# An encoder layer in split float32 on one core: weights' low parts made on GpSimd, the convolution's running sum in PSUM, the MLP's buffers in another order

## The chip, the cores and the metric

The kernel runs on one core of a Trainium2 chip. The metric is device microseconds of one execution, lower is better. Engines are named as in the profile: PE (TensorE), DVE (VectorE), ACT (ScalarE), POOL (GpSimd) and SP (SyncE), whose queue issues most DMAs.

## The reference, cut to what matters

One layer of an encoder over 512 tokens of 1024 channels, in float32. Three branches read the same normalised input, are weighted by sigmoid gates, summed, projected and added to the input; a squared-ReLU MLP follows.

```python
h = rms_norm(x, norm_mix_pre)
za, zb, q, k, v, su, sv, gl = split(h @ w_in)             # w_in: 1024 x 10240
a = za * sigmoid(zb)
a = depthwise_conv(a, conv_w) + conv_b                    # 31 taps per channel
y_a = silu(layer_norm(a, conv_ln_g, conv_ln_b)) @ w_proj_conv
y_b = rms_norm(diff_attention(q, k, v, lam, slopes)) @ w_proj_attn      # 8 heads
gv = layer_norm(gelu(sv)); y_c = (gelu(su) * (sgu_w @ gv + sgu_b)) @ w_proj_sgu
g_a, g_b, g_c = split(sigmoid(gl + b_gate))
x = x + rms_norm((g_a * y_a + g_b * y_b + g_c * y_c) @ w_out, norm_mix_post)
h = rms_norm(x, norm_ffn_pre)
x = x + rms_norm(square(relu(h @ w_ffn_up)) @ w_ffn_down, norm_ffn_post)
```

## The kernel before, in words

**Split operands.** Every float32 operand of a matmul is kept as two float32r tiles, a high part (the value rounded) and a low part (the value minus the high part). A product is three matmuls, high x high, high x low and low x high, in `mm3`. A *unit* is one PSUM bank of 128 x 512 results from one weight tile: 8 steps of the inner dimension, 24 matmuls. All matmuls of the program carry line L58 in the profile, all transposes L62.

**Weights.** The list `specs` names the 148 weight tiles of 512 KB each in the order in which they are used; here they are counted from 0. `load_to` does three things for each: a DMA on SP's queue into `w_raw` (L156), the high part on ACT (L157), the low part on DVE (L158, two inputs in SBUF). `w_raw`, `w_hi` and `w_lo` have three buffers each, so a high part can be written when PE is done with the tile three places earlier. `take(m)` loads two tiles beyond those that it hands out. In the first half of the program the tiles are: 0 to 3 the gated linear units (GLU) of the first two channel blocks, 4 and 5 the values of the first pair of heads, 6 and 7 queries and keys of head 0, up to 39 the rest of attention and the GLU, 40 to 47 `sv`, 48 to 63 `w_proj_attn` with its gates, 64 to 71 `su`, 72 to 87 `w_proj_sgu` with its gates, 88 to 93 six of the convolution's gates, and 94 to 103 `w_proj_conv` with the last two gates. Then come `w_out`, four tiles of `w_ffn_up`, and `w_ffn_down`.

**Order of the work.** PE's instructions are kept in program order. The other engines' order is set by a list scheduler over the program order; each engine then works strictly in its order, and a waiting instruction holds up all that stand behind it. The convolution runs on DVE beside everything else: `conv_taps` goes through the channel blocks, and for each makes a first product (L361) and 30 multiply-adds (L366) on a running sum `acc`, 128 x 512, in one SBUF buffer; `conv` hands out a number of these steps with a low priority.

**PSUM.** There are eight banks. `banks(ph, 4)` makes a pool with four banks with tag `a`, for the units, and four with tag `b`, for transposes, scores and small products. `bank(tag)` takes the next of its tag in turn; PE waits if the bank's last reader is not done.

**Stages.** (1) Norm, transposes, and three units in the banks `fb[0]`, `fb[1]`, `fb[2]`, in two halves of the tokens; then the sigmoid of `fb[0]` on ACT (`glu_gate`, L386), whose product with `fb[1]` is DVE's `glu_out` (L390); then a fourth unit. Beside them POOL zeroes the borders of the convolution's input (L353, L354), loads four small vectors for the attention's lambda (`bcast`, L194) and makes the distances for ALiBi (`iota`, L428). (2) Attention: for each head the scores and softmax run in step with the units of the next head, which are `proj_qk` (two units; DVE writes the low half of the keys at L459), `proj_v` for every second head, and late GLUs. A head's key unit is read twice by ACT (L458) and twice by DVE (L459) before its bank is free. (3) `sv`, with the attention's outputs turned beside it. (4) `merge` over `w_proj_attn`, the gating unit, `merge` over `w_proj_sgu`. (5) Layer norm of the convolution (`conv_norm`), its SiLU (`conv_silu`, ACT L753 and L754, DVE L755) and `merge` over `w_proj_conv`. (6) `w_out`, norms, and the first four tiles of `w_ffn_up` (`PLAIN`). (7) The rest of `w_ffn_up` as blocked products with seven multiplications in place of eight: `load_block` issues the DMAs (L909), `operand` makes sums and their two parts (ACT L930, DVE L931), `side` and `parts` make the sums of the other operand in the tile `ring` (ACT L882, DVE L883). (8) `w_ffn_down` and the last norm.

**Memory.** `fp` is the pool of stages 7 and 8. It is laid over the tiles of the pools that were closed before, in the order in which its tiles first appear: `gpo`, `f` (64 KB per partition), `ring` (33 KB), `r`, the six block buffers `aq`, `sn`. A tile waits until every older tile at its addresses has been read for the last time.

Of the kernel before, what the change touches and what calls it, by code (L numbers as in the profile page):

```python
# [16 lines left out]
P = 128  # L17
S = 512
# [30 lines left out]
def encoder_layer(ctx: ExitStack, tc: tile.TileContext, a: dict, out: bass.AP):  # L49
# [14 lines left out]
    def mk(name, bufs=1, **kw):  # L64
        return tc.tile_pool(name=name, bufs=bufs, reuse_waits="tile", **kw)

    def f32(ap):
        return ap.bitcast(F32)
# [10 lines left out]
    def cols(n, c0):  # L79
        return wv[n][:, :, c0:c0 + P]  # L80
# [39 lines left out]
    for n in range(KT):  # L120
        specs += [cols("w_in", GL + n * P)] if n >= EARLY else []
        specs += [cols("w_proj_conv", n * P)]
    xp = {"pool": None, "set": range(len(specs) + 4, len(specs) + 9)}
    for nh in range(2):
        specs += [rows("w_out", k, nh * 512) for k in range(0, KT, 2)]
# [20 lines left out]
    def load_to(n):  # L146
        while len(loaded) < min(n, gate_at[0]):
            if len(loaded) in xp["set"] and xp["pool"] is None:
                break
            src = specs[len(loaded)]  # L150
            m = src.shape[2]
            raw = wp.tile([P, 1024], F32, tag="raw", bufs=3, name="w_raw")
            p, n_ = (xp["pool"], 5) if len(loaded) in xp["set"] else (wp, 3)
            hi = p.tile([P, 1024], F32R, tag="hi", bufs=n_, name="w_hi")
            lo = p.tile([P, 1024], F32R, tag="lo", bufs=n_, name="w_lo")
            nc.sync.dma_start(raw.rearrange("p (k c) -> p k c", c=m), src)  # L156
            act.activation(hi, raw, AF.Copy)  # L157
            vec.tensor_tensor(lo, raw, f32(hi[:, :]), op=ALU.subtract)  # L158
            loaded.append((hi.rearrange("p (k c) -> p k c", c=m), lo.rearrange("p (k c) -> p k c", c=m)))

    def take(m=1, ahead=2):
        i = taken[0]
        taken[0] += m
        load_to(i + m + ahead)
        return loaded[i:i + m]
# [4 lines left out]
    hp = ctx.enter_context(mk("hp"))  # L170
    ps = {"pool": None, "a": 4, "b": 4}

    def banks(stack, na):

        ps.update(pool=stack.enter_context(mk(f"ps{na}", space=PSUM)), a=na, b=8 - na)

    def bank(tag):
        return ps["pool"].tile([P, 512], F32, tag=tag, bufs=ps[tag], name=f"ps_{tag}")

    ph = ExitStack()  # L180
    banks(ph, 4)

    ident = cp.tile([P, P], F32, tag="ident", name="ident")
    make_identity(nc, ident)
# [61 lines left out]
    def run(g):  # L246
        for _ in g:
            pass
# [108 lines left out]

    def conv_taps():
        for c in range(KT):
            acc = cvp.tile([P, S], F32, tag="acc", name="acc")  # L360
            vec.tensor_scalar(acc, apad[:, c, CK - 1:CK - 1 + S], convw[:, c, CK - 1:CK], pc("conv_b", c),  # L361
                              op0=ALU.mult, op1=ALU.add)
            yield
            for j in range(CK - 2, -1, -1):
                o = acc if j else apad[:, c, 0:S]
                vec.scalar_tensor_tensor(o, apad[:, c, j:j + S], convw[:, c, j:j + 1], acc,  # L366
                                         op0=ALU.mult, op1=ALU.add)
                yield
# [64 lines left out]

    ph.close()
    ph = ExitStack()
    banks(ph, 4)

    def proj_qk(h, got):

# [135 lines left out]
    att.close()  # L575
    ph.close()
    ph = ExitStack()
    banks(ph, 4)

    brp = big.enter_context(mk("brp"))  # L580
    sgs = ExitStack()
# [4 lines left out]
    sg_b = bcast(sp, "sg_b", a["sgu_ln_b"], D)  # L586
    gv = [sp.tile([P, D], F32, tag="gv", bufs=4, name="gv") for _ in range(TT)]

    def sv_half(nh, ws, tag):
        bs = [bank(tag) for _ in range(TT)]  # L590
        for i, w in enumerate(ws):
            for t in range(TT):
                tk = slice(t * P, (t + 1) * P)
                for k in range(2):
                    kt = 2 * i + k
                    mm3(bs[t], (hh[:, kt, tk], hl[:, kt, tk]), [x_[:, k] for x_ in w], kt == 0, kt == KT - 1)
                yield
        for t in range(TT):
            act.activation(gv[t][:, nh * 512:(nh + 1) * 512], bs[t], AF.Gelu)

    run(sv_half(0, sv_first, "a"))


    oss2 = oss.rearrange("p t h -> p (t h)")
# [3 lines left out]
    vec.tensor_tensor(orr, orr, fin, op=ALU.mult)  # L608
    bh = brp.tile([P, KT, S], F32R, tag="bh", name="bh")
    bl = brp.tile([P, KT, S], F32R, tag="bl", name="bl")  # L610
    fill = sv_half(1, take(4), "b")
    for h in range(H):
        next(fill)
        next(fill)
# [154 lines left out]
    ml = brp.tile([P, KT, S], F32R, tag="bl", name="ml")  # L769
    merge(p3, "w_proj_conv", (ch, cl), 0, last=(mh, ml), early=ga)  # L770
    c3.close()


    dp = ctx.enter_context(mk("dp", space=DRAM))
# [58 lines left out]
    fp = ctx.enter_context(mk("fp"))  # L833
    gpo = bcast(fp, "gpo", a["norm_ffn_post"], D)
    f = fp.tile([P, FT, S], F32, tag="f", name="f")
    ring = fp.tile([P, 8 * 1024 + P], F32R, tag="ring", name="ring")

    def half(j, at):
# [60 lines left out]
            vec.tensor_tensor(sums[7], B[1, 1], B[0, 1], op=ALU.subtract)  # L899
        parts(i)  # L900

    blocks = {}

    def load_block(q, name):
        if q < FT // 4:
            i, j = int(name[0]) - 1, int(name[1]) - 1
            p, tag, n_ = (wp, "raw", 3) if name == "12" else (fp, "aq", 6)
            t = p.tile([P, 1024], F32, tag=tag, bufs=n_, name="w_raw")
            nc.sync.dma_start(t.rearrange("p (k c) -> p k c", c=256),  # L909
                              rows4("w_ffn_up", 4 * j, q * 512 + i * 256))  # L910
            blocks[q, name] = t

    def operand(q, i):

        if q >= FT // 4:
# [24 lines left out]
                    pe.matmul(o[:, oc], w[sw][:, kt, xc], m[sm][:, kt], start=first and kt + x_ + p_ == 0,  # L940
                              stop=kt == 3 and p_ == 2, skip_group_check=True)

    def snap(src):
        t = fp.tile([P, S], F32, tag="sn", bufs=4, name="snap")
        act.activation(t, src, AF.Copy)
        return t

    def plus(ps_, t):
        r = fp.tile([P, S], F32, tag="r", bufs=2, name="r")
        vec.tensor_tensor(r, ps_, t, op=ALU.add)  # L950
        return r

    for n in ("11", "21", "22", "12"):
        load_block(1, n)
    operand(1, 0)
    operand(1, 1)
    side(0)
# [136 lines left out]
```

## Time and profile before

| | us |
|---|---|
| median of 3 runs (1076.57 to 1077.61) | 1076.61 |
| profiled execution, its own time | 1075.01 |
| its span, first to last instruction | 1072.9 |
| PE busy | 1054.8 |
| DVE busy | 770.5 |
| ACT busy | 550.2 |
| POOL busy | 14.1 |

A row of the timeline has the start in us from the span's start, the duration, engine, line, operation, output and inputs; in brackets stands how long the engine was idle before it and what ended the idle time. A row of the waits names who waited, for whom, the sum in us, how often, and the longest. PE's matmuls are pipelined: one of 128 x 512 is shown with 0.39 us, while the next starts 0.23 us after it.

### The profile page before, as it was taken

Reading aid. Unit: us, or ns where it says so; the run is one execution under the profiler, and the core shown is the slowest. Engines: PE = TensorE matmul, PEld = TensorE weight load, DVE = VectorE, ACT = ScalarE, POOL = GpSimd, SP = SyncE. Lnnn points to the kernel's source line nnn. Section 1 sums busy time; section 2 is a strip of 40 time slices with the busy share of each in tenths; the row PEclk is TensorE's granted clock in tenths of the full one; section 3 lists DMA queues with packets and bytes.
Section 4 is the critical chain, followed back from the end, with each engine's and each line's share of the span. In section 5 each row is a group of like instructions: output and inputs, shape, how many; then the busy total and the mean of one; then the engine's idle time right before and its main releaser. Section 6 shows DMA issues by size and latency. Waiting matters only on the chain.

```text
span 1072.9 us, 14691 instructions
## 1 busy us (share of the span) xinstructions
PE 1054.8 (98%) x5736; PEld 909.6 (85%) x5736; DVE 770.5 (72%) x1242; ACT 550.2 (51%) x868; POOL 14.1 (1%) x32
## 2 busy tenths in 40 slices
PE   8999999999999999999999999999899999999997
PEld 7989898988878888888888888889799998888885
DVE  6686878978997798998898455477988785333325
ACT  5456677776664742344222673354677775323222
POOL 3000000000000000000000000000000000000000
PEclk9999999999999999999999999999999999999999
DMA  7342332233233333322333233643434315233222
GB/s 224 82 137 63 96 98 80 79 86 91 79 99 98 100 103 97 94 79 84 93 99 98 79 92 102 230 127 137 139 99 122 96 54 189 92 99 97 98 79 79
DMA packets 135109, 111.86 MB, mean 104 GB/s; under 512 B 3957, under 2 KB 116641, under 8 KB 135040
## 3 DMA queue, kind: packets, MB, share of 16 engines
q1 hardware_dynamic: 132032, 101.73, 31.3%
q0 software_dynamic: 2288, 7.63, 2.2%
q10 hardware_dynamic: 720, 1.57, 0.4%
q8 instruction: 45, 0.74, 0.3%
q14 instruction: 24, 0.20, 0.1%
HBM read 102.52 MB, written 4.19 MB: 99 GB/s over the span
## 4 chain that ended last, share of the span: by engine, by line
PE 91%; DVE 4%; ACT 2%; DMA 1%; issue 1%; SPq 0%; DVEq 0%; ACTq 0%
PE ps_a L58 68%; PE ps_b L58 20%; PE ps_b L62 3%; DMA w_raw<-in_w_in_dram 1%; DVE w_lo L158 0%; DVE w_lo L931 0%; ACT y L745 0%; ACT w_hi L157 0%; DMA w_raw<-in_w_ffn_up_dram 0%; DVE jk L821 0%; PE ps_a L62 0%; ACT jk L819 0%; SPq L281 0%; DVE hs L297 0%; DVE wk L816 0%
## 5 line engine op out<-in xcount | busy, mean ns | idle before, releaser
L157 ACT ACTIVATE w_hi<-w_raw 128x1024 fp32r<-128x1024 f32 x148 | 156.5, 1058 | 272.2 <-PE ps_a L58 181.7
L158 DVE TENSOR_TENSOR w_lo<-w_raw,w_hi 128x1024 fp32r<-128x1024 f32 x148 | 180.7, 1222 | 97.1 <-ACT w_hi L157 96.7
L58 PE MATMUL ps_a<-hh,w_hi 128*128 128x512 f32 (+1 forms) x536 | 205.4, 385 | 0.0
L58 PE MATMUL ps_a<-hh,w_lo 128*128 128x512 f32 (+1 forms) x536 | 203.0, 381 | 0.0
L58 PE MATMUL ps_a<-hl,w_hi 128*128 128x512 f32 (+1 forms) x536 | 202.6, 380 | 0.0
L366 DVE SCALAR_TENSOR_TENSOR acc<-apad,convw,acc 128x512 f32<-128x512 f32 x232 | 173.8, 749 | 5.0
L58 PEld LDWEIGHTS ps_a<-hh,w_lo 128*128 128x128 f32 x536 | 100.3, 188 | 19.6
L58 PEld LDWEIGHTS ps_a<-hh,w_hi 128*128 128x128 f32 x536 | 100.5, 188 | 18.3
L58 PEld LDWEIGHTS ps_a<-hl,w_hi 128*128 128x128 f32 x536 | 100.4, 188 | 18.2
L58 PE MATMUL ps_a<-w_hi,ring 128*128 128x512 f32 x256 | 83.7, 389 | 0.0
L58 PE MATMUL ps_b<-w_hi,ring 128*128 128x512 f32 x256 | 83.7, 389 | 0.0
L58 PE MATMUL ps_a<-ring,w_hi 128*128 128x256 f32 x336 | 58.2, 277 | 0.6 <-ACT w_hi L930 0.6
L58 PEld LDWEIGHTS ps_a<-w_hi,ring 128*128 128x128 f32 x256 | 48.1, 188 | 9.9
L58 PEld LDWEIGHTS ps_b<-w_hi,ring 128*128 128x128 f32 x256 | 48.0, 188 | 9.9
L1012 DVE TENSOR_TENSOR ring<-f,ring 128x1024 fp32r<-128x1024 f32 x16 | 19.6, 1225 | 48.0 <-ACT ring L1011 48.0
L58 PEld LDWEIGHTS ps_a<-ring,w_hi 128*128 128x128 f32 x336 | 50.6, 188 | 0.8 <-ACT w_hi L930 0.8
L58 PE MATMUL ps_a<-h2h,w_lo 128*128 128x256 f32 x176 | 48.7, 277 | 1.8 <-DVE w_lo L931 1.8
L58 PE MATMUL ps_a<-w_lo,ring 128*128 128x512 f32 x128 | 49.9, 390 | 0.1
L58 PE MATMUL ps_b<-w_lo,ring 128*128 128x512 f32 x128 | 49.8, 389 | 0.0
L58 PE MATMUL ps_a<-w_hi,hh 128*128 128x256 f32 (+1 forms) x160 | 49.7, 311 | 0.0
L58 PE MATMUL ps_a<-h2h,w_hi 128*128 128x256 f32 x176 | 48.9, 278 | 0.5 <-ACT w_hi L930 0.5
L58 PE MATMUL ps_a<-h2l,w_hi 128*128 128x256 f32 x176 | 48.8, 277 | 0.0
(274 smaller groups left out, 2213.9 us busy)
## 6 DMA issues: line engine op xcount, KB each, us to landing
w_raw<-in_w_in_dram SPq DMA_DIRECT2D x80, 512.0 KB, 3.7
w_raw<-in_w_ffn_up_dram SPq DMA_DIRECT2D x32, 512.0 KB, 4.4
w_raw<-in_w_ffn_down_dram SPq DMA_DIRECT2D x32, 512.0 KB, 3.6
w_raw<-in_w_proj_attn_dram SPq DMA_DIRECT2D x8, 512.0 KB, 4.1
w_raw<-in_w_proj_sgu_dram SPq DMA_DIRECT2D x8, 512.0 KB, 4.0
w_raw<-in_w_proj_conv_dram SPq DMA_DIRECT2D x8, 512.0 KB, 4.0
w_raw<-in_w_out_dram SPq DMA_DIRECT2D x8, 512.0 KB, 3.6
xx<-in_x_dram SPq DMA_DIRECT2D x4, 512.0 KB, 7.6
```

Source lines behind the costliest of these rows:

```text
L58: return tc.keep_in_program_order(nc.tensor.matmul(*args, **kw))
L62: return tc.keep_in_program_order(nc.tensor.transpose(*args, **kw))
L157: act.activation(hi, raw, AF.Copy)
L158: vec.tensor_tensor(lo, raw, f32(hi[:, :]), op=ALU.subtract)
L366: vec.scalar_tensor_tensor(o, apad[:, c, j:j + S], convw[:, c, j:j + 1], acc, op0=ALU.mult, op1=ALU.add)
L1012: vec.tensor_tensor(lo, src, f32(hi), op=ALU.subtract)
```

## The change

Three things are changed.

1. The low parts of weights 4 to 99 are made on POOL, by the same operation (L158 before, L160 now). Weights 0 to 3 and 100 on stay on DVE.
2. The running sum `acc` of the convolution stands in PSUM, in a pool of one bank that is open from the start to the end of stage 5. Until then the units have three banks `a` in place of four; `b` keeps four. The first half of `sv`, which needs four banks at once, takes three `a` and one `b`. From stage 6 on there are four and four as before. Without `acc`, the pools behind it lie 2 KB lower in SBUF.
3. In `fp`, the block buffers, `sn` and `r` stand ahead of `ring`, and the first four block loads are called before the four `PLAIN` units rather than after them.

```diff
+    on_pool = set(range(4, len(specs) - 4))
...
-            vec.tensor_tensor(lo, raw, f32(hi[:, :]), op=ALU.subtract)
+            (pool if len(loaded) in on_pool else vec).tensor_tensor(lo, raw, f32(hi[:, :]), op=ALU.subtract)
...
-    def banks(stack, na):
+    def banks(stack, na, nb=4):
-        ps.update(pool=stack.enter_context(mk(f"ps{na}", space=PSUM)), a=na, b=8 - na)
+        ps.update(pool=stack.enter_context(mk(f"ps{na}", space=PSUM)), a=na, b=nb)
...
+    tp = ExitStack()
+    tapp = tp.enter_context(mk("tap", space=PSUM))
     ph = ExitStack()
-    banks(ph, 4)
+    banks(ph, 3)
...
-            acc = cvp.tile([P, S], F32, tag="acc", name="acc")
+            acc = tapp.tile([P, S], F32, tag="acc", name="acc")
...
-    run(sv_half(0, sv_first, "a"))
+    run(sv_half(0, sv_first, "aaab"))
...
     c3.close()
+    ph.close()
+    tp.close()
+    ph = ExitStack()
+    banks(ph, 4)
...
     f = fp.tile([P, FT, S], F32, tag="f", name="f")
+    blocks = {}
+    def load_block(q, name):
...
+    def snap(src):
...
+    for n in ("11", "21", "22", "12"):
+        load_block(1, n)
+    fp.tile([P, S], F32, tag="sn", bufs=4, name="snap")
+    fp.tile([P, S], F32, tag="r", bufs=2, name="r")
     ring = fp.tile([P, 8 * 1024 + P], F32R, tag="ring", name="ring")
...
-    for n in ("11", "21", "22", "12"):
-        load_block(1, n)
     operand(1, 0)
```

PE's order is the same but for the banks. On POOL the low parts stand between its other work. In the first stage, before, its row runs from the load of the convolution's taps through the borders (`apad`), the vectors of lambda (`lq`, `lk`) and the distances (`dist`) to the load for stage 3 (`sg_g`):

```order
L333 DMA cw<-in_conv_w_dram 31x1024
L353 MEMSET apad 128x8x15
L354 MEMSET apad 128x8x15
L194 DMA lq_537<-in_lam_q_dram 128x64
L194 DMA lk_539<-in_lam_k_dram 128x64
L194 DMA lq_547<-in_lam_q_dram 128x64
L194 DMA lk_549<-in_lam_k_dram 128x64
L428 IOTA dist 128x896
L194 DMA sg_g<-in_sgu_ln_g_dram 128x1024
```

Now, at the same place (the first two low parts are those of weights 4 and 5):

```order
L338 DMA cw<-in_conv_w_dram 31x1024
L160 TENSOR_TENSOR w_lo<-w_raw,w_hi 128x1024
L358 MEMSET apad 128x8x15
L359 MEMSET apad 128x8x15
L199 DMA lq_540<-in_lam_q_dram 128x64
L160 TENSOR_TENSOR w_lo<-w_raw,w_hi 128x1024
L199 DMA lk_542<-in_lam_k_dram 128x64
L199 DMA lq_550<-in_lam_q_dram 128x64
L199 DMA lk_552<-in_lam_k_dram 128x64
L433 IOTA dist 128x896
L160 TENSOR_TENSOR w_lo<-w_raw,w_hi 128x1024 x37
L199 DMA sg_g<-in_sgu_ln_g_dram 128x1024
```

The borders, the vectors and the distances now stand behind one or two low parts, and the load for stage 3 behind 37 more.

ACT's order moves in the heads. In head 2, whose units are the next head's queries and keys and a pair of values, its row before was (`e` the exponentials, `at` the scaled scores, `qh` and `kk` the high parts of queries and keys, `ath` and `vh` those of the turned scores and the values):

```order
L449 ACTIVATE qh_1529<-ps_a_1424 64x512
L508 ACTIVATE at_1574<-e_1557,r_1560 128x512
L458 ACTIVATE kk_1614<-ps_a_1539 64x512
L157 ACTIVATE w_hi_1620<-w_raw_1619 128x1024
L501 ACTIVATE e_1567,l_1568<-ps_b_1562,m_1565 128x512
L501 ACTIVATE e_1591,l_1592<-ps_b_1586,m_1589 128x512
L501 ACTIVATE e_1601,l_1602<-ps_b_1596,m_1599 128x512
L458 ACTIVATE kk_1614<-ps_a_1539 64x512
L71 ACTIVATE ath_1468<-ps_b_1652 128x4x128
```

Now the same work stands in this order:

```order
L454 ACTIVATE qh_1532<-ps_a_1427 64x512
L506 ACTIVATE e_1570,l_1571<-ps_b_1565,m_1568 128x512
L513 ACTIVATE at_1577<-e_1560,r_1563 128x512
L506 ACTIVATE e_1594,l_1595<-ps_b_1589,m_1592 128x512
L463 ACTIVATE kk_1617<-ps_a_1542 64x512
L506 ACTIVATE e_1604,l_1605<-ps_b_1599,m_1602 128x512
L513 ACTIVATE at_1611<-e_1594,r_1597 128x512
L159 ACTIVATE w_hi_1623<-w_raw_1622 128x1024
L463 ACTIVATE kk_1617<-ps_a_1542 64x512
L71 ACTIVATE ath_1471<-ps_b_1655 128x4x128
```

The first half of the keys has two exponentials and one scaling more ahead of it, and the second half has the next weight's high part just ahead of it.

More of the change, by code (lines that the diff above doesn't have):

```diff
@@ L435, in encoder_layer @@
     ph = ExitStack()
-    banks(ph, 4)
+    banks(ph, 3)
     def proj_qk(h, got):
@@ L577, in encoder_layer @@
     ph = ExitStack()
-    banks(ph, 4)
+    banks(ph, 3)
     brp = big.enter_context(mk("brp"))
@@ L587, in encoder_layer, with sv_half @@
     gv = [sp.tile([P, D], F32, tag="gv", bufs=4, name="gv") for _ in range(TT)]
-    def sv_half(nh, ws, tag):
-        bs = [bank(tag) for _ in range(TT)]
+    def sv_half(nh, ws, tags):
+        bs = [bank(tag) for tag in tags]
         for i, w in enumerate(ws):
@@ L610, in encoder_layer @@
     bl = brp.tile([P, KT, S], F32R, tag="bl", name="bl")
-    fill = sv_half(1, take(4), "b")
+    fill = sv_half(1, take(4), "bbbb")
     for h in range(H):
@@ L835, in encoder_layer @@
     f = fp.tile([P, FT, S], F32, tag="f", name="f")
+    blocks = {}
+    def load_block(q, name):
+        if q < FT // 4:
+            i, j = int(name[0]) - 1, int(name[1]) - 1
+            p, tag, n_ = (wp, "raw", 3) if name == "12" else (fp, "aq", 6)
+            t = p.tile([P, 1024], F32, tag=tag, bufs=n_, name="w_raw")
+            nc.sync.dma_start(t.rearrange("p (k c) -> p k c", c=256),
+                              rows4("w_ffn_up", 4 * j, q * 512 + i * 256))
+            blocks[q, name] = t
+    def snap(src):
+        t = fp.tile([P, S], F32, tag="sn", bufs=4, name="snap")
+        act.activation(t, src, AF.Copy)
+        return t
+    for n in ("11", "21", "22", "12"):
+        load_block(1, n)
+    fp.tile([P, S], F32, tag="sn", bufs=4, name="snap")
+    fp.tile([P, S], F32, tag="r", bufs=2, name="r")
     ring = fp.tile([P, 8 * 1024 + P], F32R, tag="ring", name="ring")
@@ L900, in side @@
         parts(i)
[L902 to L911, printed above, removed]
     def operand(q, i):
@@ L941, in product @@
                               stop=kt == 3 and p_ == 2, skip_group_check=True)
[L943 to L946, printed above, removed]
     def plus(ps_, t):
```

## The prediction

> **What bounds the kernel now.** First the page's totals, then its chain that ended last, then the waits of PE alone.
>
> ```profile
> span 1072.9 us, 14691 instructions
> PE 1054.8 (98%) x5736; PEld 909.6 (85%) x5736; DVE 770.5 (72%) x1242; ACT 550.2 (51%) x868; POOL 14.1 (1%) x32
> ```
> ```profile
> PE 91%; DVE 4%; ACT 2%; DMA 1%; issue 1%; SPq 0%; DVEq 0%; ACTq 0%
> ```
>
> PE is busy for all but 18.1 us, and 91% of the chain is PE. So relief of DVE has no price by itself; only PE's idle time can be won, and each new wait of PE is lost. Where the 18.1 us lie is told by PE's waits and by the windows (length, then PE, PEld, DVE, ACT, POOL busy):
>
> ```profile
> PE ps_a L58 <- DVE w_lo L931: 3.5, 3, 1.8
> PE ps_b L62 <- DVE hs L297: 2.2, 2, 1.7
> PE ps_b L58 <- DVE zero L269: 1.5, 1, 1.5
> ```
> ```profile
> PE ps_b L58 <- DVE kk L459: 0.5, 1, 0.5
> ```
> ```profile
> 311.00:740.00 429.00, 427.94 (x2013) 356.69 (x2014) 326.38 (x526) 187.69 (x256) 4.11 (x7) 1.00 0.35 105
> 740.00:770.00 30.00, 25.45 (x214) 24.43 (x213) 25.61 (x24) 18.06 (x24) 0.00 (x0) 1.00 0.45 150
> ```
>
> From 311 to 740 us PE stands still for 1.06 us, though DVE is busy 76% of that time. Of the rest 4.55 us lie where the MLP begins (740 to 770; `w_lo` of L931 has 3.5 of them), and 0.5 us where head 0 waits for `kk`. Nothing else is within this change's reach: `hs` and `zero` belong to the opening norm.
>
> **Low parts on POOL.** 96 of 148 leave DVE; the sum stays where PE is unless one comes late. The page has DVE's row; the lines of POOL have no operation of two tensors, the nearest is a written tile:
>
> ```profile
> L158 DVE TENSOR_TENSOR w_lo<-w_raw,w_hi 128x1024 fp32r<-128x1024 f32 x148 | 180.7, 1222 | 97.1 <-ACT w_hi L157 96.7
> ```
> ```profile
> 25.45 0.53 POOL L194 DMA_DIRECT2D lk<-in_lam_k_dram  x1
> 25.99 0.90 POOL L428 IOTA dist<- 128x896 f32 x1
> ```
>
> POOL passes 896 elements in 0.90 us, so 1024 in 1.03. One pass is the lower bound, three (two reads, one write, nothing overlapped) 3.1 us the upper. I take two, 2.05 us, one for each input, as `iota` is nearest. [...]
>
> Is that in time? Typical is weight 55, a gate of stage 4:
>
> ```profile
> 386.31 1.06 ACT L157 ACTIVATE w_hi<-w_raw 128x1024 fp32r<-128x1024 f32 x1 [0.55 <-PE ps_a L58]
> ```
> ```profile
> 392.18 0.39 PE L58 MATMUL ps_a<-hh,w_lo 128*128 128x512 f32 x1
> ```
>
> High part done at 387.37, low part wanted at 392.18: 4.8 us, cover for the whole range. Weight 95, whose high part ACT's SiLU work makes late, is the exception:
>
> ```profile
> 631.90 1.23 DVE L158 TENSOR_TENSOR w_lo<-w_raw,w_hi 128x1024 fp32r<-128x1024 f32 x1 [0.17 <-ACT w_hi L157]
> ```
> ```profile
> 632.83 0.39 PE L58 MATMUL ps_a<-cl,w_hi 128*128 128x512 f32 x1
> 633.18 0.50 PE L58 MATMUL ps_a<-ch,w_lo 128*128 128x512 f32 x1
> ```
>
> The high part ends ahead of this row's 0.17 us, at 631.7, and DVE starts at 631.90. PE steps by 0.23 us, so it wanted the low part at 633.06 and already waited 0.1. On POOL it ends at 631.90 + 2.05 = 633.95: **+0.9 us** (0 at 1.15 us a part, 1.9 at 3.1).
>
> Leaving DVE helps at head 0, where a low part stood ahead of the second `kk`:
>
> ```profile
> 65.52 1.23 DVE L158 TENSOR_TENSOR w_lo<-w_raw,w_hi 128x1024 fp32r<-128x1024 f32 x1 [0.33 <-ACT w_hi L157]
> 66.77 0.69 DVE L459 TENSOR_TENSOR kk<-ps_a,kk 64x512 fp32r<-64x512 f32 x1
> ```
>
> With 1.23 us off DVE's row the 0.5 us wait goes, **-0.45 us** (0 to -0.5). What is late next there is nothing: the next head's units follow.
>
> **The sum in PSUM.** The 232 multiply-adds below and their 8 first products are taken to last as long with the sum in PSUM; no row shows a DVE result in PSUM (the nearest, L390 above 512 elements from PSUM, is quoted below at 0.69 us, no slower). If each took half as long again, DVE would gain 0.5 x 174 = 87 us of work and still lose 96 x 1.222 = 117 us of low parts. Nothing on PE's path.
>
> ```profile
> L366 DVE SCALAR_TENSOR_TENSOR acc<-apad,convw,acc 128x512 f32<-128x512 f32 x232 | 173.8, 749 | 5.0
> ```
>
> **Three banks: the fourth unit.** `fb[0]` to `fb[2]` now fill all three, so the fourth unit waits for the sigmoid of `fb[0]`, which stands on ACT behind weight 5's high part and a table load, in this order still:
>
> ```profile
> 32.80 1.06 ACT L157 ACTIVATE w_hi<-w_raw 128x1024 fp32r<-128x1024 f32 x1 [1.82 <-PE ps_a L58]
> 35.68 1.06 ACT L157 ACTIVATE w_hi<-w_raw 128x1024 fp32r<-128x1024 f32 x1 [1.82 <-PE ps_a L58]
> 36.76 1.28 ACT L386 ACT_TABLE_LOAD   x1
> 38.05 1.09 ACT L386 ACTIVATE sg<-ps_a 128x512 f32<-128x512 f32 x2
> ```
> ```profile
> 36.41 0.50 PE L58 MATMUL ps_a<-hh,w_hi 128*128 128x512 f32 x1
> ```
> ```profile
> 38.68 0.69 DVE L390 TENSOR_TENSOR apad<-ps_a,sg 128x512 f32<-128x512 f32 x1 [0.35 <-ACT sg L386]
> ```
>
> PE started this unit at 36.41; DVE, which waits for the same sigmoid, got it at 38.68. PE gets it then too: **+2.27 us**. No cover: weight 5's high part waits for PE itself.
>
> Behind it lies a longer chain, of which these rows are the start and the ends:
>
> ```profile
> 39.29 1.08 DVE L430 SCALAR_TENSOR_TENSOR al<-dist 128x896 f32<-128x896 f32 x1
> ```
> ```profile
> 46.29 0.42 DVE L72 TENSOR_TENSOR vl<-ps_a,vh 128x256 fp32r<-128x256 f32 x1
> ```
> ```profile
> 41.98 0.28 PE L58 MATMUL ps_a<-w_hi,hh 128*128 128x256 f32 x1
> ```
>
> Weight 4's high part ends at 33.86, so POOL's low part at 35.9; borders and one vector are taken at 1.1 us, weight 5's low part ends at 39.1, three vectors of 0.53 and `iota`'s 0.90 at 41.6, where before it ended at 26.89. So `al` starts at 41.6, not 39.29. The first low half of the values (`vl`) ended 7.4 us after `al` began; now five more taps of 0.75 stand between and one low part of 1.22 fewer: 41.6 + 7.4 + 2.5 = 51.5. It frees the bank that the fourth value tile needs. Value tiles begin at 41.98, and each takes 24 matmuls of about 0.12 (half the width of a unit's, whose step is 0.23): the fourth is wanted at 41.98 + 8.6 + 2.27 = 52.9. That is 1.4 us of cover, gone when a low part takes 2.75 us, since two lie in the chain; I take nothing (0 to +0.7).
>
> **Three banks: the heads.** With three, a value tile after `kk` takes `kk`'s bank. In head 2:
>
> ```profile
> 140.86 0.72 ACT L508 ACTIVATE at<-e,r 128x512 f32<-128x512 f32 x1
> 141.61 0.59 ACT L458 ACTIVATE kk<-ps_a 64x512 fp32r<-64x512 f32 x1
> 142.10 1.05 ACT L157 ACTIVATE w_hi<-w_raw 128x1024 fp32r<-128x1024 f32 x1
> 143.05 0.67 ACT L501 ACTIVATE e<-ps_b,m 128x512 f32<-128x512 f32 x1
> ```
> ```profile
> 146.71 0.69 DVE L459 TENSOR_TENSOR kk<-ps_a,kk 64x512 fp32r<-64x512 f32 x1
> ```
> ```profile
> 147.81 0.28 PE L58 MATMUL ps_a<-w_hi,hh 128*128 128x256 f32 x1
> ```
>
> Before, the bank was free at 147.40, used at 147.81. By the order now, two exponentials and a scaling (0.67 + 0.67 + 0.72) precede the first `kk` at 141.61, and another of each and the high part (0.67 + 0.72 + 1.05) the second: it starts at 141.61 + 2.06 + 0.59 + 2.44 = 146.70, DVE ends at 148.0 or, if an exponential waits for its maximum, later: +0.2 to +0.5 us. Head 4 is the same shape, head 0 has more room. [...] I take **+0.7 us** (0 to +2.5).
>
> **The MLP's buffers.** Before, the first block load waited for PE, and ACT for the load:
>
> ```profile
> SPq L909 <- PE ps_a L58: 10.9, 1, 10.9
> ```
> ```profile
> 746.54 0.60 ACT L851 ACTIVATE r<-ps_a 128x512 f32<-128x512 f32 x1 [1.46 <-PE ps_a L58]
> 747.67 1.06 ACT L930 ACTIVATE w_hi<-w_raw 128x1024 fp32r<-128x1024 f32 x1 [0.54 <-DMA w_raw<-in_w_ffn_up_dram]
> ```
> ```profile
> 735.84 1.27 DVE L821 SCALAR_TENSOR_TENSOR jk<-wk,rs_r,gpre 128x1024 f32<-128x1024 f32 x1
> ```
>
> The buffer now lies over `gpost` and `gpre2`, last read by DVE's last L821, at 737.1: the load leaves then, not after PE's units. But ACT's order is unchanged: its high part still stands behind the second L851, which PE releases at 746.5. So it comes 0.6 us earlier, at 747.1, and the full DVE behind it with it: **-0.6 us** (0 to -0.7).
>
> **Sum**: 2.27 + 0.9 + 0.7 - 0.45 - 0.6 = +2.8 us on the profiled 1075.01. That execution is 1.6 under the median of the runs, on which I put the forecast: 1076.6 + 2.8 = **1079.4 us**. A measurement can tell 0.2%, 2.15 us: faster is under 1074.5, slower over 1078.8.
>
> **Rivals.**
> *Covered, no change (0.20):* POOL makes a part in one pass, so weight 95 and the heads cost nothing: 2.27 - 1.05 = +1.2, 1077.8. For it: `iota`'s rate. Against: two inputs.
> *POOL and DVE hold each other up (0.18):* an operation of DVE with two SBUF inputs, as L509 in the heads, waits out a low part. In heads 2 and 4 it stands ahead of the second `kk`: 2 x 2.05 more, and 0.7 in the opening; from 0.6 us of delay on, head 4 shows it too. 1079.4 + 4.1 - 0.7 + 0.7 = 1083.5. For it: 34 parts (weights 6 to 39) x 2.05 = 70 us lie in the some 240 us of the heads. Against: units and running sums have one input in PSUM. [...]
> *Faster (0.08):* the early load lets ACT make the block's high part before its L851 rows, DVE starts on the sums while PE is in the `PLAIN` units, and the 4.55 us at the MLP's start go: 2.27 - 0.5 - 4.55 = -2.8, 1073.8. It decides when L930 starts ahead of the second L851, 746.5. For it: DVE is busy 25.6 of 30 us there, so it is DVE that PE waits for, and an earlier start is all it lacks. Against: ACT's order.
>
> **The numbers.** My case has 0.54, from +1.5 to +4, two thirds of it over the bound. Slower: 0.36 + 0.18 = 0.54; same: 0.18 + 0.20 = 0.38; faster 0.08. The range leaves out the faster case and the far end of the second rival: 1076.6 to 1083.5.
>
> **What would show it.** PE's waits would list L58 for ACT `sg` with 2.2 us near 36.4, and L58 for POOL `w_lo` once with about 0.9 us near 635; head 0's `kk` would be gone, and L931's sum down by 0.6. A POOL row under 1.2 us or over 2.75, a wait for `sg` under 1 us, or DVE's L509 well over 747 ns would prove a step wrong.

## The result, and the profile after

The changed kernel took 1089.8 us as median of four runs (1085.24 to 1094.5), the kernel before 1076.65: a ratio of 1.0126 (95% interval 1.0101 to 1.0151). It is slower, as forecast, but the forecast was 1079.4 and its range ended at 1083.5. The profiled execution took 1089.73 us, with a span of 1088.0, 15.1 us more than that of before.

One thing is needed to read the times below: executions of one kernel differ, by 8 us among 28 of the kernel before (1074.82 to 1082.65) and by 9 among the four of the changed one (why, as far as the traces show it, stands at the end). Medians are therefore given with the interval of their ratio, and places are compared in the traces.

The page's totals, its chain that ended last, and the first of PE's waits, after:

```profile
span 1088.0 us, 14738 instructions
PE 1061.1 (98%) x5736; PEld 913.7 (84%) x5736; DVE 708.4 (65%) x1146; ACT 549.4 (50%) x868; POOL 253.4 (23%) x128
```
```profile
PE 88%; DVE 5%; issue 3%; ACT 2%; DMA 1%; POOL 1%; SPq 0%; DVEq 0%; POOLq 0%; ACTq 0%
```
```profile
PE ps_a L58 <- POOL w_lo L160: 3.6, 2, 2.4
PE ps_a L58 <- DVE w_lo L950: 3.1, 2, 1.8
PE ps_b L62 <- DVE hs L302: 2.5, 3, 1.6
PE ps_a L58 <- ACT sg L391: 2.2, 1, 2.2
PE ps_b L58 <- DVE atl L72: 1.6, 1, 1.6
```

DVE lost 62 us of work, and nothing was won by it. Waits for POOL (3.6), for the sigmoid (2.2) and for the last head's `atl` (1.6) are new; the wait for `kk` is gone. But PE's busy time rose too, by 6.3 us for the same 5736 instructions: some of them ran slower.

PE issues the same instructions in the same order in both kernels, so the start of the n-th in one trace minus the start of the n-th in the other is its lag, and the places where the lag steps are the places where time was lost:

| place | start before | start after | lag after it | step |
|---|---|---|---|---|
| fourth unit's start | 36.41 | 38.69 | 2.28 | +2.28 |
| within that unit, to 43 us | | | 3.78 | +1.50 |
| head 0, keys | 68.86 | 72.15 | 3.29 | -0.49 |
| heads 1 to 6 | | | 3.29 | 0 |
| last head's turned scores and product | 307.82 | 313.87 | 6.05 | +2.76 |
| weight 55, high and low part | 392.18 | 401.41 | 9.23 | +3.18 |
| the matmuls behind it, to 405 us | | | 10.80 | +1.57 |
| convolution's norm, `y` turned | 613.00 | 624.38 | 11.38 | +0.58 |
| weight 95 | 633.18 | 645.75 | 12.57 | +1.19 |
| MLP's start | 757.99 | 770.01 | 12.01 | -0.56 |
| the matmuls at 781 to 787 us | | | 14.75 | +2.74 |
| to the end | | | 15.07 | +0.32 |

Three of the steps are no waits. The windows of the changed kernel there (length, then busy PE, PEld, DVE, ACT, POOL, and behind them the granted clock) show PE busy, but for the end of a stall in the second, at about half its clock:

```profile
39.00:43.00 4.00, 4.00 (x12) 3.09 (x11) 1.94 (x3) 0.13 (x1) 3.20 (x5) 0.57 0.73 117
401.00:405.00 4.00, 3.59 (x9) 2.87 (x10) 3.89 (x6) 0.00 (x0) 2.70 (x2) 0.57 0.46 137
781.00:787.00 6.00, 6.00 (x29) 6.00 (x30) 4.07 (x5) 1.40 (x2) 0.00 (x0) 0.51 0.67 204
```

Each of them follows on a stall of PE: of 2.22 us, of 2.42, and at the MLP's start of 1.81 us behind shorter ones.

The groups of POOL's low part and of DVE's operations that share the time with it, first of the changed kernel, then two of before:

```profile
L160 POOL TENSOR_TENSOR w_lo<-w_raw,w_hi 128x1024 fp32r<-128x1024 f32 x96 | 239.4, 2497 | 405.2 <-ACT w_hi L159 395.8 <-issue 6.4 <-PE ps_b L62 3.0
L371 DVE SCALAR_TENSOR_TENSOR acc<-apad,convw,acc 128x512 f32<-128x512 f32 x232 | 174.7, 753 | 5.9
L514 DVE SCALAR_TENSOR_TENSOR at<-e,c,at 128x512 f32<-128x512 f32 x32 | 29.6, 924 | 4.0 <-ACT at L513 2.4
L511 DVE TENSOR_TENSOR c<-r,nlam 128x1 f32<-128x1 f32 x32 | 15.6, 486 | 0.6
```
```profile
L509 DVE SCALAR_TENSOR_TENSOR at<-e,c,at 128x512 f32<-128x512 f32 x32 | 23.9, 747 | 1.9 <-ACT at L508 1.4
L506 DVE TENSOR_TENSOR c<-r,nlam 128x1 f32<-128x1 f32 x32 | 5.0, 158 | 0.6
```

A product of 128 x 1 elements took 158 ns and takes 486 on average. The multiply-add with its sum in PSUM (one input in SBUF) kept its time, 753 for 749 ns; the two operations above with both inputs in SBUF did not (924 for 747, 486 for 158). How that comes about is seen in the last head, in the rows of POOL, DVE and PE:

```profile
304.01 4.75 POOL L160 TENSOR_TENSOR w_lo<-w_raw,w_hi 128x1024 fp32r<-128x1024 f32 x2 [9.59 <-ACT w_hi L159]
```
```profile
304.03 2.39 DVE L511 TENSOR_TENSOR c<-r,nlam 128x1 f32<-128x1 f32 x1
306.35 0.74 DVE L371 SCALAR_TENSOR_TENSOR acc<-apad,convw,acc 128x512 f32<-128x512 f32 x1
307.00 2.31 DVE L514 SCALAR_TENSOR_TENSOR at<-e,c,at 128x512 f32<-128x512 f32 x1
```
```profile
309.37 0.65 PE L62 MATMUL ps_b<-ident,at 128*128 128x128 f32 x4 [0.87 <-DVE at L514]
313.87 0.50 PE L58 MATMUL ps_b<-atl,vh 128*128 128x512 f32 x1 [1.56 <-DVE atl L72]
```

POOL's two low parts fill 304.01 to 308.76. The 128 x 1 product, begun 0.02 us after the first, ends when that ends (2.39 us for 0.16 of work); the multiply-add with one input in SBUF then passes in 0.74 beside the second; L514, with two, ends 0.55 us after the second. The last head has no units left beside it, so PE waits: +2.76 us.

In stage 4 it goes both ways. Rows of DVE, POOL, ACT and PE around weight 55:

```profile
392.21 3.96 DVE L647 TENSOR_TENSOR gv<-gv,sg_b 128x1024 f32<-128x1024 f32 x2
```
```profile
390.55 3.40 POOL L160 TENSOR_TENSOR w_lo<-w_raw,w_hi 128x1024 fp32r<-128x1024 f32 x1 [5.38 <-ACT w_hi L159]
398.29 3.07 POOL L160 TENSOR_TENSOR w_lo<-w_raw,w_hi 128x1024 fp32r<-128x1024 f32 x1 [4.34 <-ACT w_hi L159]
```
```profile
395.06 2.20 ACT L648 ACTIVATE gvh<-gv 128x1024 fp32r<-128x1024 f32 x2 [4.59 <-DVE gv L647]
397.17 1.04 ACT L159 ACTIVATE w_hi<-w_raw 128x1024 fp32r<-128x1024 f32 x1
```
```profile
401.41 0.79 PE L58 MATMUL ps_a<-hh,w_lo 128*128 128x512 f32 x1 [2.42 <-POOL w_lo L160]
```

DVE's two sums for the gating unit's norm (1.22 us each without POOL) take 3.96; ACT waits 4.59 us for them, and weight 55's high part stands behind ACT's work on them; POOL's low part comes after it and takes 3.07. PE waits 0.19 for the high part and 2.42 for the low one.

ACT's order has moved here too. Before, weight 55's high part (386.31) stood between ACT's two operations on the norm (L643, now L648); now it stands behind both:

```profile
384.69 1.06 ACT L643 ACTIVATE gvh<-gv 128x1024 fp32r<-128x1024 f32 x1 [1.68 <-DVE gv L642]
388.55 1.06 ACT L643 ACTIVATE gvh<-gv 128x1024 fp32r<-128x1024 f32 x1 [0.61 <-DVE gv L642]
```

An estimate from these rows: DVE's sums lost 1.6 us to POOL and POOL's low part 0.7 to DVE, 2.3 of the 3.18 us; the rest is left to the moved order and to POOL's longer instruction.

Ahead of `y` an operation on 128 x 1 with two inputs in SBUF, which took 0.22 us before, ends when POOL's low part ends:

```profile
609.93 0.22 DVE L213 SCALAR_TENSOR_TENSOR rs_s<-rs_v,rs_r 128x1 f32<-128x1 f32 x1
```
```profile
619.12 2.39 POOL L160 TENSOR_TENSOR w_lo<-w_raw,w_hi 128x1024 fp32r<-128x1024 f32 x1 [6.91 <-ACT w_hi L159]
```
```profile
620.89 0.64 DVE L218 SCALAR_TENSOR_TENSOR rs_s<-rs_v,rs_r 128x1 f32<-128x1 f32 x1
```

### The profile page after: what moved, and what is told of

The parts are those of the page before. It is cut to its first block, busy times and chain, and to the rows that moved or that the text cites. A ratio compares the mean times of both kernels' runs of the same rounds, so it can differ in the third digit from the quotient of the medians.

```text
span 1088.0 us, 14738 instructions
## 1 busy us (share of the span) xinstructions
PE 1061.1 (98%) x5736; PEld 913.7 (84%) x5736; DVE 708.4 (65%) x1146; ACT 549.4 (50%) x868; POOL 253.4 (23%) x128
## 3 DMA queue, kind: packets, MB, share of 16 engines
q10 hardware_dynamic: 720, 1.57, 0.4%
## 4 chain that ended last, share of the span: by engine, by line
PE 88%; DVE 5%; issue 3%; ACT 2%; DMA 1%; POOL 1%; SPq 0%; DVEq 0%; POOLq 0%; ACTq 0%
PE ps_a L58 65%; PE ps_b L58 20%; PE ps_b L62 2%; DMA w_raw<-in_w_in_dram 1%; POOL w_lo L160 1%; DVE acc L371 0%; DVE w_lo L950 0%; DVE at L514 0%; DVE jk L830 0%; PE ps_a L62 0%; ACT jk L828 0%; SPq L286 0%; ACT w_hi L159 0%; DVE hs L302 0%; DVE wk L825 0%
## 5 line engine op out<-in xcount | busy, mean ns | idle before, releaser
L160 POOL TENSOR_TENSOR w_lo<-w_raw,w_hi 128x1024 fp32r<-128x1024 f32 x96 | 239.4, 2497 | 405.2 <-ACT w_hi L159 395.8
L160 DVE TENSOR_TENSOR w_lo<-w_raw,w_hi 128x1024 fp32r<-128x1024 f32 x52 | 63.5, 1222 | 78.6 <-ACT w_hi L159 78.6
```

The source lines that it names most:

```text
L160: (pool if len(loaded) in on_pool else vec).tensor_tensor(lo, raw, f32(hi[:, :]), op=ALU.subtract)
```

## The experiments

Three runs took the change apart, three asked whether POOL and DVE exclude each other, two what the fourth unit and the clock cost, and three went on from what part 3 of the change brings. The *exclusion theory*, read from the last head's rows (2.39 us for 0.16 of work): a DVE instruction with two inputs in SBUF and a low part on POOL don't run together; the later waits for the end of the other. Its rivals: POOL's rate alone, and the banks with the order that they move.

**Low parts on POOL alone.** The sum stays in SBUF, with four banks and the old buffers.

```diff
-            vec.tensor_tensor(lo, raw, f32(hi[:, :]), op=ALU.subtract)
+            (pool if len(loaded) in on_pool else vec).tensor_tensor(lo, raw, f32(hi[:, :]), op=ALU.subtract)
```

> Low parts of weights 4 to 99 on POOL, running sum in SBUF, four banks, old MLP buffers. Exclusion theory (a DVE instruction with two SBUF inputs and a POOL low part do not run together; the later waits for the other's end): the 240 taps have two SBUF inputs now, so their mean leaves 749 ns and passes 1000 ns; from 311 to 587 us DVE's 240 us less 60 of low parts plus POOL's 118 is 298 in 276, so DVE binds there: 1095 to 1110 us. Rival, POOL's rate alone (2.4 us a part, no exclusion): the taps stay at 749 ns, only weight 95 is late, by 1.2 us: 1076 to 1079. Rival, the banks and the moved order: no wait of the fourth unit, 1076 to 1078.

Measured: 1118.02 us, ratio 1.0379 (1.035 to 1.0408). The group of the taps, the chain and the longest of PE's waits:

```profile
L367 DVE SCALAR_TENSOR_TENSOR acc<-apad,convw,acc 128x512 f32<-128x512 f32 x232 | 257.9, 1112 | 6.2
```
```profile
PE 63%; DVE 26%; issue 5%; ACT 4%; POOL 1%; DMA 0%; DVEq 0%; POOLq 0%; ACTq 0%
```
```profile
PE ps_b L58 <- DVE kk L460: 5.5, 1, 5.5
```

With two inputs in SBUF the taps went from 749 to 1112 ns: 84 us more on DVE, which now has 26% of the chain. The two rivals fall, which gave at most 1079. My upper end of 1110 was too low: I had counted one stage in which DVE binds, and it also held up head 0, the gating unit and the norm. The sum in PSUM is what makes low parts on POOL bearable: 41 us lost here, 13 in the full change.

**The sum in PSUM and three banks alone.** Low parts on DVE, old buffers.

> Running sum in PSUM and three banks, low parts on DVE, old MLP buffers. Exclusion theory: only the fourth unit's wait of 2.2 us with 1.5 us at half clock behind it, nothing at the last head and in stage 4: 1078 to 1081 us. Rival, the banks and the moved order cost what was lost at 305 to 314 and 391 to 404 us: those losses (2.8 and 4.3 us) are here too, 1084 to 1090. Rival, POOL's rate alone: as the exclusion theory.

Measured: 1083.2 us, ratio 1.0058 (1.0039 to 1.0076). Among its waits of PE:

```profile
PE ps_a L58 <- ACT sg L391: 2.2, 1, 2.2
PE ps_a L58 <- DVE kk L464: 1.5, 2, 0.8
```

No step of the lag at the last head, in stage 4 or at weight 95, so the banks did not cause those. But the expectation of both theories, 1078 to 1081, missed something: the lag steps by 0.96 us in head 2 and by 1.00 in head 4, where a value tile waits for the bank of `kk`, as the prediction had it. In the full change this wait does not appear: DVE's second `kk` of head 2 ends at 150.51 there, for a bank that PE takes at 151.05. No low part stands ahead of `kk` on DVE there (here one does, at 147.67), but ACT's order is another too; which of the two takes the wait away was not separated.

**The MLP's buffers alone.**

> The MLP's buffers in the new order, nothing else. All theories: the block's first high part starts 0.5 to 0.6 us earlier and the sum of PE's waits for L931 falls by as much: 1075.8 to 1076.4 us. If PE's clock is halved after the stall at the MLP's start, up to 2.8 us more.

Measured: 1076.03 us, ratio 0.9994 (0.9978 to 1.0011): no change that can be told. In the trace the high part starts when the second relu ends, 0.5 us earlier than before (747.67), and the lag is -0.50 where PE's stall there ends (768.81 before, 768.31 here):

```profile
746.68 0.60 ACT L871 ACTIVATE r<-ps_a 128x512 f32<-128x512 f32 x1 [1.46 <-PE ps_a L58]
747.17 1.05 ACT L939 ACTIVATE w_hi<-w_raw 128x1024 fp32r<-128x1024 f32 x1
```

**Some low parts back on DVE.** The full change without the weights whose parts lie in the last head, the gating unit's norm and the convolution's norm and first units.

```diff
-    on_pool = set(range(4, len(specs) - 4))
+    on_pool = set(range(4, len(specs) - 4)) - {40, 41, *range(50, 57), *range(93, 100)}
```

> The changed kernel with the low parts of weights 40, 41, 50 to 56 and 93 to 99 back on DVE. Exclusion theory: the losses at the last head (2.8 us), in stage 4 (2.9 of wait and 1.6 of half clock), at y (0.6) and at weight 95 (1.2) go, the fourth unit's 2.2 and 1.5 stay: PE runs 5 to 6 us behind the kernel before at the end, 1079 to 1083. Rival, the banks and the moved order: 1087 to 1091, as with all parts on POOL. Rival, POOL's rate alone: the wait at weight 95 and the one in stage 4 go, the last head's 2.8 us stays: 1081 to 1085.

Measured: 1080.74 us, ratio 1.0025 (1.0006 to 1.0044). After head 0 the lag stays at 3.5 us until the MLP: 80 low parts on POOL cost nothing, and the steps of 2.76, 3.18, 0.58 and 1.19 are gone with the other 16. PE's waits list no POOL. The time is the one that the exclusion theory gave, and the last head's step, which POOL's rate alone would have left, is not there. The path to that time was not as expected: PE is 2.9 us behind where the MLP's stalls end, not 5 to 6, and in the profiled execution it ends 7.7 behind, at the slower of two rates of the MLP's products (last section). At weight 55 this run has ACT's old order back as well, so there it does not tell the exclusion from the order.

**Two and four instructions for a low part.** If the exclusion is by instruction, a shorter one on POOL must shorten DVE's wait, though POOL's work stays the same.

```diff
-            (pool if len(loaded) in on_pool else vec).tensor_tensor(lo, raw, f32(hi[:, :]), op=ALU.subtract)
+            if len(loaded) in on_pool:
+                for c in (0, 512):
+                    pool.tensor_tensor(lo[:, c:c + 512], raw[:, c:c + 512], f32(hi[:, c:c + 512]), op=ALU.subtract)
+            else:
+                vec.tensor_tensor(lo, raw, f32(hi[:, :]), op=ALU.subtract)
```

> The changed kernel with each low part on POOL made by two instructions of 512 columns. Exclusion by instruction: the longest wait of a DVE instruction falls from 2.4 to about 1.2 us (the 128 x 1 product ahead of the scaled scores of the last head takes 1.3 at most in place of 2.39, where POOL's two instructions don't follow without a gap), and the 2.8 us at the last head fall to 1 to 2. Rival, DVE waits until POOL has nothing left to do, or the loss comes from POOL's rate: the 2.4 us and the 2.8 us stay.

Measured: 1082.81 us, ratio 1.0043 (1.0022 to 1.0064). The next run took quarters (`range(0, 1024, 256)`), and the bank `b` of a run below:

> The changed kernel with each low part on POOL made by four instructions of 256 columns and the fourth unit in a bank b. If DVE waits for one POOL instruction at a time: the 128 x 1 product takes at most 0.7 us (2.39 whole, about 1.3 in halves) and means under 230 ns (486 whole, 258 in halves); the last head loses under 0.4 us (2.76 whole, 0.59 in halves), stage 4 under 0.9 (3.2 and 1.17). PE ends 1 to 2 us behind the kernel before where the clock stays full: 1076 to 1078. If POOL pays a fixed price for an instruction: its busy time grows over 245 us and weight 95 is late again by 1 us or more.

Measured: 1078.75 us, ratio 1.0000 (0.998 to 1.002). The groups of POOL's low part and of the 128 x 1 product, of the run in halves and of the run in quarters:

```profile
L162 POOL TENSOR_TENSOR w_lo<-w_raw,w_hi 128x512 fp32r<-128x512 f32 x192 | 258.5, 1369 | 381.9 <-ACT w_hi L159 372.7 <-issue 6.2 <-PE ps_b L62 2.8
```
```profile
L515 DVE TENSOR_TENSOR c<-r,nlam 128x1 f32<-128x1 f32 x32 | 8.3, 258 | 0.6
```
```profile
L162 POOL TENSOR_TENSOR w_lo<-w_raw,w_hi 128x256 fp32r<-128x256 f32 x384 | 296.1, 804 | 342.6 <-ACT w_hi L159 334.2 <-issue 5.9 <-PE ps_b L62 2.5
```
```profile
L515 DVE TENSOR_TENSOR c<-r,nlam 128x1 f32<-128x1 f32 x32 | 7.7, 241 | 0.6
```

| | whole | halves | quarters |
|---|---|---|---|
| POOL, all low parts, us | 239.4 | 258.5 | 296.1 |
| longest 128 x 1 product, us | 2.39 | 1.29 | 0.74 |
| step of the lag, last head | 2.76 | 0.59 | none |
| weight 55 | 3.18 | 1.17 | none |
| `y` | 0.58 | 0.81 | 0.75 |
| weight 95 | 1.19 | none | -0.25 |

The longest wait of DVE is one POOL instruction each time (2.39, 1.29 and 0.74 us, where POOL's instruction takes 2.50, 1.37 and 0.80 on average), while POOL's total rises. That settles it for the last head: DVE waits for an instruction, not for the engine, and POOL's rate is not what cost it. The bank `b` is not the reason either: with it and whole parts (a run below) the last head steps by 2.76 and weight 55 by 3.24.

At weights 55 and 95 a second thing helps: a unit begins with the first columns' part and no longer needs the whole (in quarters PE takes weight 55's low part from 393.20 on, and POOL ends it at 395.43). So these two runs do not isolate the exclusion's share there. At `y` shorter instructions do not help, since the small operations still meet one or two of them (0.79 us in halves, 0.39 and 0.59 in quarters, where 0.22 was taken before).

The other account of the last run was half right: POOL does pay for each instruction (239.4 us in 96, 258.5 in 192, 296.1 in 384: 0.20 us for each one more), but weight 95 is not late. The marks of that run were missed by little: 0.74 us for 0.7, a mean of 241 ns for 230, and 1078.75 us for at most 1078.

**PE kept busy ahead of the fourth unit.**

```diff
     (w,) = take(1)
+    hold = bank("b")
+    for _ in range(10):
+        pe.matmul(hold, hh[:, 0, 0:P], hh[:, 0], start=True, stop=True)
     b = bank("a")
```

> The changed kernel with ten matmuls of 128 x 512 whose results are not used (10 x 0.227 = 2.27 us) ahead of the fourth unit, so that PE is busy while it waits for the sigmoid. If a stall of PE is what halves the clock: the granted clock from 39 to 43 us is 1.00 and the unit ends 1.5 us earlier, with its start at 38.7 as it was: 1.5 us less than the changed kernel, all else equal. Rival, the half clock there comes from something else (the time since the start, POOL's or the DMAs' work): 0.93 for 40 to 60 us as before and no gain.

Measured: 1086.95 us, ratio 1.0095 (1.0062 to 1.0129). The windows at 39 us of this run, and behind its later stall in stage 4:

```profile
39.00:43.00 4.00, 4.00 (x19) 3.30 (x18) 1.88 (x3) 0.06 (x1) 3.19 (x5) 1.00 0.71 114
399.00:406.00 7.00, 6.19 (x15) 4.91 (x16) 5.80 (x9) 0.00 (x0) 3.10 (x2) 0.51 0.51 150
```

The unit starts at 38.72 as it did at 38.69, the clock is whole, and the first value tile starts at 44.21 in place of 45.88: 1.67 us less. In the four traces with this stall and nothing in the gap (the changed kernel, the banks alone, some parts back, halves) the granted clock there is 0.57, 0.60, 0.57 and 0.60; in this one it is 1.00. Here it is PE's stall that halves the clock. The profiled execution, the slowest of the four, lost more at its stall in stage 4, where nearly all of the 7 us shown are at half clock; the ratios of the medians differ in the right direction (1.0095 here, 1.0126 for the changed kernel), but their intervals overlap and do not show the gain.

**The fourth unit in a bank `b`** (one word: `bank("b")`).

> The changed kernel with the fourth unit in a bank b. My account: its start goes back from 38.7 to 36.4 us and the half clock behind it goes, so 2.3 + 1.5 = 3.8 us less than the changed kernel, if the value tiles are not late behind it. Rival, the longer chain on POOL (two low parts, borders, distances) makes a value tile late once the unit starts early: 1 to 2 us of the gain are given back near 50 us.

Measured: 1085.31 us, ratio 1.0075 (1.0051 to 1.0099). The lag after head 0 is 0.34 in place of 3.29 us: both the wait and the half clock are gone, and 0.5 are given back at the second value tile, which waits for the product L395 (in the run in quarters, 1.1). PE's row at weight 55 and the window behind it, in this run:

```profile
398.52 0.50 PE L58 MATMUL ps_a<-hh,w_lo 128*128 128x512 f32 x1 [2.42 <-POOL w_lo L160]
```
```profile
399.00:403.00 4.00, 4.00 (x20) 3.27 (x19) 3.86 (x7) 0.00 (x0) 1.82 (x1) 1.00 0.67 198
```

The same stall of 2.42 us, and here the clock stays whole, 1.00 where the changed kernel had 0.57 over 401 to 405: it was halved behind this stall in one profiled execution and not in the other.

**On from the MLP's buffers.** The first block's operands are called ahead of the plain units, and ACT's first high part is ordered ahead of the first relu (an order for the scheduler, no wait). Low parts on DVE, four banks.

> The kernel before with the MLP's buffers in the new order, the first block's operands called ahead of the four plain units, and ACT's first high part ordered ahead of the first relu. If the MLP's start lacks only an earlier start of DVE (the rival of the prediction that ended faster): the high part is done by 742 us, DVE starts on its low part at 744 in place of 748.8, and of PE's 4.55 us there 3 to 4.5 go: 1072 to 1073.6 us. If DVE is held by its own order or by the other loads: 0.5 to 1 us, 1075.5 to 1076.

Measured: 1075.74 us, ratio 0.9990 (0.9971 to 1.001). It fell short: the time is the one given for a DVE held by its own order, but the lock was another. ACT's first high part in that run:

```profile
746.45 1.06 ACT L931 ACTIVATE w_hi<-w_raw 128x1024 fp32r<-128x1024 f32 x1 [7.41 <-PE ps_a L58]
```

First in ACT's order, it waited for PE all the same: its buffer of `w_hi` still held the weights of a plain unit. ACT's order, on which the prediction had rested, was one of two locks that opened at almost the same time. The next run puts these two parts into a stretch of `ring` that is used late:

> As the run with ACT's first high part ahead of the first relu, but with that block's two parts in a stretch of the ring that is used late, since in that run the high part waited until 746.45 us for a buffer that a plain unit held. If that buffer was the lock: the high part is done before 743 us, DVE's low part starts at 744.4 in place of 747.5, and PE's waits for L931's low parts (2.3 us left) lose 1 to 2 us: 1074 to 1074.8 us as median. If the second operand's buffer, held by the next plain unit, is the next lock: 0 to 0.5 us less.

```profile
744.15 1.06 ACT L934 ACTIVATE ring<-w_raw 128x1024 fp32r<-128x1024 f32 x1 [4.85 <-PE ps_a L58]
745.25 1.23 DVE L938 TENSOR_TENSOR ring<-w_raw,ring 128x1024 fp32r<-128x1024 f32 x1 [0.58 <-ACT ring L934]
```

Measured: 1076.36 us (forecast 1074 to 1074.8) where before took 1078.28 beside it, ratio 0.9979 (0.9958 to 1.0000); the lowest of its 12 executions 1073.10, of the 23 of before 1075.09. The part now waits for the first plain unit (the expectation said before 743), DVE starts 2.3 us earlier than in the run ahead, and PE leads the kernel before by 1.77 us behind its stalls there (0.77 in the run ahead). The last of these runs also keeps PE busy there:

```diff
+        if q == 1:
+            hold = bank("b")
+            for _ in range(10):
+                pe.matmul(hold, h2h[:, 0, 0:P], h2h[:, 0], start=True, stop=True)
         product(be, q, 4, quarter(1, t2), False)
```

> As the run with the first block's parts in the ring, with ten matmuls whose results are not used (2.27 us) ahead of the fifth product of the first block, where PE stood still for 0.6 and 1.8 us. If PE's stall there is what halves the clock in some executions: none of the executions has a half clock at the MLP's start, so the group of times 1.5 us above the lowest goes; median 1073.2 to 1075 us with the lowest as before, 1073.1. If the slower rate of the blocked products (57 matmuls in 6.71 in place of 6.46 us, 4.5 us in all) comes with that stall too, the group 6 us above the lowest goes as well; if not, it stays.

Measured: 1075.66 us, ratio 0.9984 (0.9964 to 1.0003); six executions at 1073.1 to 1073.5 us and six at 1077.9 to 1078.1. In the run ahead seven of twelve lay 1.5 us above a lower group (at 1074.6 to 1074.7 and at 1079.4 to 1079.5); here none does. The upper group stays, so it has another cause, and with it the median misses the forecast. These two are the lowest versions of the study. By the lowest executions they gain 2 us; by the medians the gain is at the edge of what can be told.

## Why the prediction was wrong, step by step

- **What bounds the kernel:** right. DVE lost 62 us, PE's waits decided.
- **A low part on POOL, 2.05 us:** within its bounds, too small. Undisturbed it took 2.40 us (4.75 for the two above), 2.50 on average with what it waited for DVE.
- **"4.8 us, cover for the whole range" for weight 55:** this is the step that failed, and at the very weight that was picked as typical. It took the high part's time as given and counted only POOL's duration. But ACT's order moved, and the high part stood behind both operations on the gating unit's norm, which wait for DVE's two-input operations, which waited for POOL. +3.18 us, some 2.3 of it by the exclusion. The prediction had read the moved order in head 2 and took the old one here.
- **The rival of POOL and DVE:** it was right, with a chance of 0.18, and its place was wrong. It was priced in heads 2 and 4, where PE has units to go on with and the lag shows nothing; it came where PE has nothing else, in the last head (2.76) and at weight 55, and at `y` (0.58). It should have been a term of the sum, which gave it nothing in these places: the rival took the conflict for every DVE operation with two inputs in SBUF, as an assumption, and only the place that PE waits for was to be found. The argument against it, that the running sums have one input in PSUM, is right as far as it goes: the taps kept their time (753 for 749 ns), and with the sum in SBUF (1112 ns) the loss was 41 us in place of 13.
- **Fourth unit, +2.27:** 2.28. But the price of a stall had no term for the clock behind it. +1.50 here, +1.57 behind weight 55, +2.74 at the MLP's start: 5.8 us in all. The last is chance and no price of the change: the kernel before has the same stalls there (1.28 and 1.81 us), and its profiled execution, 1.6 us under the median, kept its clock (1.00 over 755 to 785 us). The fastest execution of the changed kernel, 1085.24 us with a mean granted clock of 0.997 (0.992 in the profiled one), suggests that the range is missed without most of the half clock too.
- **Weight 95, +0.9:** 1.19; with 2.40 in place of 2.05 the same working gives 1.24.
- **Head 0, -0.45:** -0.49.
- **Heads 2 and 4, +0.7:** 0. The wait is real with low parts on DVE (1.96 with the banks alone), and is not there in the full change, where DVE has less to do and ACT another order; the two parts of the change were not weighed together here. No run shows the far end of this term's range, +2.5: in heads 1 to 6 the lag of the changed kernel steps by 0, and with low parts on DVE heads 2 and 4 lost 0.96 and 1.00.
- **The opening's longer chain, 0:** 0 behind the late unit; 0.5 to 1.1 us once the unit is early.
- **The sum in PSUM, no cost:** right, 753 for 749 ns in the 232 steps.
- **MLP's buffers, -0.6:** -0.56, for the reason given, and for a second one that the runs found.

The terms that were in the sum gave 2.8 us and measured 2.28 + 1.19 + 0 - 0.49 - 0.56 = 2.4; that they come so near is in part luck, since the 0.7 of the heads was not there and weight 95 cost 0.3 more. That the kernel became slower, as forecast, they carry for these 2.4 of 15.07 us only. What was left out was 2.76 + 3.18 + 0.58 = 6.5 us where POOL's instructions meet DVE's, and 5.8 us at half clock. The first is shown for the last head by putting parts back and by halves and quarters; at `y` and weight 55 it is read from the rows, at weight 55 together with the moved order. The second is shown by keeping PE busy at the fourth unit and, on the kernel before with its buffers moved, at the MLP's start; behind weight 55 the same cause is argued from the window.

## What to carry to other kernels

Work moved to POOL is not paid by POOL's duration alone: count each DVE instruction with two inputs in SBUF that may meet it as lasting a whole POOL instruction longer (2.39 us for 0.16 in the last head), and look for those on which PE waits with nothing else to do; short POOL instructions (the last head's step went from 2.76 to 0.59 us with halves, but `y` did not gain) and operands in PSUM (taps of 753 ns in place of 1112) were the remedies here. A stall of PE of about 2 us had a second price behind it, 1.50, 1.57 and 2.74 us in the changed kernel, in some executions; harmless matmuls in the gap took it away in both runs that tried them (a granted clock of 1.00 over 39 to 43 us; at the MLP's start 1.00 over 755 to 785, and none of twelve executions 1.5 us above a lower group). Where a list scheduler sets the order, moving work to another engine moves the order of all engines: read the new order at each place that is priced. If an earlier load or another order brings nothing, look at the buffer that the next step writes.

## What the runs showed of the hardware

The clock was halved for 3.4 us (a granted clock of 0.57 over 39 to 43 us, behind PE's stall of 2.22 us that ended at 38.69) to nearly 7 (0.51 over 399 to 406 in the run with PE kept busy, with a stall of 2.41) behind stalls of 1.8 to 2.4 us, and not behind each of them (1.00 over 399 to 403 in the run with the fourth unit in a bank `b`, behind 2.42 us). In the run with the MLP's buffers alone, whose waits of PE for that block were 1.3 us and shorter, it was 0.94 over 755 to 785 us, where before had 1.00.

The blocked products of the MLP run at one of two rates at a granted clock of 1.00. The windows of before and of the run with some parts back on DVE:

```profile
820.00:880.00 60.00, 60.00 (x531) 60.00 (x531) 49.44 (x48) 42.25 (x59) 0.00 (x0) 1.00 0.26 80
```
```profile
820.00:880.00 60.00, 60.00 (x512) 60.00 (x511) 47.40 (x47) 41.85 (x58) 0.00 (x0) 1.00 0.25 80
```

531 or 512 matmuls in 60 us. From 770 to 890 us the slower rate costs 4.3 us by these counts (120 x 19 / 531; the last expectation has 4.5). It was found in six of the 13 profiled executions, with and without a half clock ahead of it. The upper group of the run above fits it: the profiled execution of the ring run, which had this rate and no half clock at the MLP's start, took 1077.99 us. Its cause stays open.

Writing PSUM costs DVE's first product of a channel block, a multiply and add of one tensor with two columns, 0.80 us where it took 0.54 into SBUF, while the multiply-add of two tensors keeps its time (753 for 749 ns):

```profile
396.09 0.80 DVE L366 TENSOR_SCALAR acc<-apad,convw,pcol 128x512 f32<-128x512 f32 x1
```
```profile
40.42 0.54 DVE L361 TENSOR_SCALAR acc<-apad,convw,pcol 128x512 f32<-128x512 f32 x1
```
